# Masking the attention scores on VectorE in the operation that takes their minimum, with new plan prices and an earlier first w_oc blob

## The chip, the cores and the metric

The kernel runs on one core of a Trainium2 chip. A core has five engines that run their own instruction queues side by side: TensorE (PE in the profile; PEld is its weight loads), VectorE (DVE), ScalarE (ACT), GpSimd (POOL) and SyncE (SP), which here only issues transfers. They work on SBUF, TensorE writes its results to PSUM, and DMA engines move data between SBUF and HBM. The metric is the device time of one launch in microseconds (us), lower is better.

## What is computed

One decoder layer for 512 tokens of width 2048 in fp32: a modulation vector, a norm, one combined projection, a short convolution beside attention with 8 query heads in 2 key groups, an output projection, and a feed-forward part. The change lies in attention. Cut to what matters:

```python
def masked_softmax(s, mask):
    s = jnp.where(mask, s, jnp.finfo(jnp.float32).min)
    p = jax.nn.softmax(s, axis=-1)
    return jnp.where(mask, p, 0.0)
...
    # per block of 128 query rows; gathered and window branches, 8 heads each
    s = jnp.einsum('bgrqd,bgqkd->bgrqk', qbk, k_sel).astype(jnp.float32) * scale
    p = masked_softmax(s, (pos <= t[:, None])[:, :, None])
    o_slc = jnp.einsum('bgrqk,bgqkd->bgrqd', p.astype(v_sel.dtype), v_sel)
...
    s = jnp.einsum('bgrqd,bgkd->bgrqk', qbk, kw).astype(jnp.float32) * scale
    p = masked_softmax(s, wmask)
    o_win = jnp.einsum('bgrqk,bgkd->bgrqd', p.astype(vw.dtype), vw)
```

With 512 tokens the selection takes every block, and the window covers everything before it, so both branches have the same causal mask: key position not after the query row.

## The kernel before

The whole layer is one function, `hybrid_layer`, in three parts. Each part is recorded by a class `Order` instead of being issued at once: every call becomes a node with a price (`price`, lines 93 to 114, in us), and `emit` lays the nodes out in time by these prices, by their dependences and by the number of buffers, and then issues them in the order of planned start. Each engine works its own queue strictly in that order. So a wrong price does not change what is computed, but it changes which instruction stands behind which. All calls pass through line 122, so nearly all instructions carry that line in the profile, and one reads them by the names of their tiles.

1. The first plan (up to line 936): modulation (`w_ada` blobs, a multiply with a running sum on VectorE each, tile `t<-wa,cs`), projections, convolution, and the queries. `weights` (line 368) brings one weight blob of 512 KB: a transfer from SP's queue into `raw` (3 buffers), a copy to a rounded high half by ScalarE and a subtraction for the low half by VectorE into `wh` (2 buffers). TensorE computes each product as three products of halves (`mm3`).
2. The second plan (lines 948 to 1096): attention and the convolution's half of the output projection. This is where the change acts. `attention(g, qb)` handles one key group (2) and one block of 128 query rows (4): for two branches and four heads, three score products into a PSUM tile `s` (3 buffers), a fourth product that adds the causal mask to its last 128 columns (`s<-mask_r,ident_r`, line 995), the negated row maximum `nm` on VectorE (line 998), and on ScalarE the exponential into `p` with the row sum (line 1001). `p` is in SBUF with 8 buffers. That makes 64 such score tiles, 16 each of 128, 256, 384 and 512 columns. Then VectorE scales `p`, TensorE transposes it into `pt`, both others split it into `tt`, and TensorE multiplies with the values into `pv`. `out_conv(m)` (line 962), 16 times, is independent work: 24 products of 512 columns into `pw` with a blob of `w_oc`; the planner may put it wherever TensorE would idle, since it has the last place among the lanes (`lane(2)`). Query heads 4 to 7 (`head`, tiles `rt`, `q`) are rotated on VectorE among the first four blocks.
3. The third plan (from line 1101): the attention half of the output projection and the feed-forward part, tiles `pf`.

Between two plans nothing is planned: the second plan starts all engines at zero, whatever the first has left in their queues. `wanted()` marks nodes that are to be done 10 us before the first plan's end would ask for them. The price of a score maximum is taken from its output, one column, in the kernel before: 0.1 us at any width (line 106). The mask product is priced 0.06 us (line 101).

## Time and profile before

| | us |
|---|---|
| median of 3 runs (2114.53 to 2116.34) | 2115.92 |
| the profiled execution, whole | 2115.59 |
| its span, first to last instruction | 2113.8 |
| first score product of attention (start of the second plan's work on PE) | 554.25 |
| first product of the third plan | 759.22 |

| engine | busy us | share of the span |
|---|---|---|
| PE | 2068.4 | 98% |
| PEld | 1923.7 | 91% |
| DVE | 1885.7 | 89% |
| ACT | 1007.3 | 48% |
| POOL | 128.2 | 6% |

A product is written in the profile as its output tile, its two inputs and the columns that it streams. Products overlap, so the busy time of PE counts a product's latency too; how fast PE really goes is read from the distance between starts. A row of a window shows for each engine its busy time and number of instructions in that stretch, then the granted clock of TensorE as a share (1.00 is full), and the load of the DMA engines. The chain of waits follows the work that ended last back from the end, each step to what released it.

### The profile page before, as it was taken

Reading aid. Unit: us, or ns where it says so; the run is one execution under the profiler, and the core shown is the slowest. Engines: PE = TensorE matmul, PEld = TensorE weight load, DVE = VectorE, ACT = ScalarE, POOL = GpSimd, SP = SyncE. Lnnn points to the kernel's source line nnn. Section 1 sums busy time; section 2 is a strip of 40 time slices with the busy share of each in tenths; the row PEclk is TensorE's granted clock in tenths of the full one; section 3 lists DMA queues with packets and bytes.
Section 4 is the critical chain, followed back from the end, with each engine's and each line's share of the span. In section 5 each row is a group of like instructions: output and inputs, shape, how many; then the busy total and the mean of one; then the engine's idle time right before and its main releaser. Section 6 shows DMA issues by size and latency. Waiting matters only on the chain.

```text
span 2113.8 us, 38166 instructions
## 1 busy us (share of the span) xinstructions
PE 2068.4 (98%) x15070; PEld 1923.7 (91%) x15070; DVE 1885.7 (89%) x3039; ACT 1007.3 (48%) x1471; POOL 128.2 (6%) x244
## 2 busy tenths in 40 slices
PE   8999999999999999999999999999999999999997
PEld 6888787898777779999999999999999999999997
DVE  7999888888987556999999999999899999999997
ACT  5432433222455434766666666666444333334354
POOL 0000000000000001022211112111000000000000
PEclk8999999999999999999999999999999999999998
DMA  8897588888321144467666676668976466476442
GB/s 335 340 340 249 181 297 325 315 288 311 138 80 41 51 141 154 135 215 225 210 204 207 207 217 200 208 206 288 332 268 211 167 242 220 145 255 237 150 172 90
DMA packets 144130, 454.17 MB, mean 215 GB/s; under 512 B 15824, under 2 KB 20176, under 8 KB 143952
## 3 DMA queue, kind: packets, MB, share of 16 engines
q1 hardware_dynamic: 108816, 386.72, 53.0%
q0 software_dynamic: 34048, 63.98, 9.6%
q8 instruction: 118, 1.93, 0.4%
q10 hardware_dynamic: 1088, 1.05, 0.1%
q14 instruction: 60, 0.49, 0.1%
HBM read 383.53 MB, written 68.16 MB: 214 GB/s over the span
## 4 chain that ended last, share of the span: by engine, by line
PE 72%; DVE 9%; DMA 4%; ACT 2%; issue 2%; DVEq 0%; POOL 0%; SPq 0%; ACTq 0%
PE pf L122 55%; PE ps L122 11%; PE pw L122 3%; DMA rw<-in_w_f 1%; PE pv L122 1%; DVE hl L122 1%; DVE t L122 1%; DVE x L122 1%; PE s L122 1%; DMA wa<-in_w_ada 1%; PE pt L122 1%; DMA raw<-in_cmp_w 1%; DVE nm L122 1%; DVE wh L122 1%; DMA tk<-g 1%
## 5 line engine op out<-in xcount | busy, mean ns | idle before, releaser
L122 PE MATMUL pf<-tk,hl 128*128 128x256 f32 x10704 | 1223.3, 277 | 3.0 <-DVE hl L122 2.2
L122 PEld LDWEIGHTS pf<-tk,hl 128*128 128x128 f32 x10704 | 1219.9, 188 | 5.3 <-DVE hl L122 3.5
L122 ACT ACTIVATE hl<-rw 128x1024 fp32r<-128x1024 f32 x269 | 285.5, 1062 | 324.9 <-PE pf L122 280.1
L122 DVE TENSOR_TENSOR hl<-rw,hl 128x1024 fp32r<-128x1024 f32 (+2 forms) x351 | 336.5, 968 | 29.4 <-ACT hl L122 29.2
L122 ACT ACTIVATE hl<-sg 128x1024 fp32r<-128x1024 f32 x180 | 191.1, 1062 | 220.3 <-PE pf L122 172.8
L122 PE MATMUL ps<-h_m,wh 128*128 128x512 f32 x1080 | 252.0, 390 | 0.0
L122 DVE SCALAR_TENSOR_TENSOR t<-wa,cs 128x1024 bf16<-128x1024 f32 x192 | 234.5, 1221 | 16.1 <-DMA wa<-in_w_ada 13.8
L122 PEld LDWEIGHTS ps<-h_m,wh 128*128 128x128 f32 x1080 | 201.1, 188 | 41.5 <-DVE wh L122 0.3
L122 ACT ACTIVATE wh<-raw 128x1024 fp32r<-128x1024 f32 (+1 forms) x106 | 112.7, 1063 | 243.8 <-PE ps L122 215.7
L122 DVE TENSOR_TENSOR hl<-sg,hl 128x1024 fp32r<-128x1024 f32 (+2 forms) x193 | 188.1, 986 | 25.3 <-ACT hl L122 25.3
L122 PE MATMUL ps<-h,wh 128*128 128x512 f32 x840 | 198.7, 392 | 3.4 <-ACT h L122 2.3
L122 PEld LDWEIGHTS ps<-h,wh 128*128 128x128 f32 x840 | 157.7, 189 | 37.0 <-ACT h L122 2.7
L122 DVE TENSOR_TENSOR wh<-raw,wh 128x1024 fp32r<-128x1024 f32 (+1 forms) x106 | 129.9, 1225 | 21.2 <-ACT wh L122 19.9
L122 DVE TENSOR_TENSOR sg<-sg,rw 128x1024 f32<-128x1024 f32 x120 | 146.1, 1217 | 0.2
L122 DVE SCALAR_TENSOR_TENSOR x<-pf,mod,x 128x256 f32<-128x256 f32 (+1 forms) x280 | 131.8, 485 | 14.5 <-PE pf L122 12.8
L122 POOL DMA_DIRECT2D g<-gt x192 | 101.2, 532 | 379.7 <-ACT hl L122 222.1
L122 PE MATMUL pw<-mix,wh 128*128 128x512 f32 x384 | 109.7, 405 | 0.0
L122 DVE TENSOR_TENSOR sg<-rw 128x1024 f32<-128x1024 f32 x60 | 73.2, 1220 | 16.7 <-DMA rw<-in_w_f 14.0
L122 ACT ACTIVATE t<-t 128x512 f32<-128x512 f32 (+3 forms) x131 | 74.9, 572 | 21.1 <-DVE t L122 18.8
L122 PEld LDWEIGHTS pw<-mix,wh 128*128 128x128 f32 x384 | 69.6, 190 | 11.0 <-issue 0.5
L122 DVE TENSOR_TENSOR rw<-rw 128x1024 f32<-128x1024 f32 x60 | 73.0, 1217 | 0.0
L122 ACT ACTIVATE gt<-t 128x512 fp32r<-128x512 f32 x96 | 60.3, 630 | 22.6 <-DVE t L122 17.7
(215 smaller groups left out, 1802.1 us busy)
## 6 DMA issues: line engine op xcount, KB each, us to landing
rw<-in_w_f SPq DMA_DIRECT2D x263, 512.0 KB, 3.9
wa<-in_w_ada SPq DMA_DIRECT2D x192, 512.0 KB, 6.0
tk<-g SPq DMA_DIRECT2D x114, 512.0 KB, 6.2
g<-gt POOLq DMA_DIRECT2D x192, 256.0 KB, 4.1
raw<-in_w_conv SPq DMA_DIRECT2D x32, 512.0 KB, 4.3
x<-in_xt SPq DMA_DIRECT2D x16, 512.0 KB, 7.2
raw<-in_w_kv SPq DMA_DIRECT2D x16, 512.0 KB, 4.4
raw<-in_w_cv SPq DMA_DIRECT2D x16, 512.0 KB, 4.5
```

Of the source, the lines that this page charges most:

```text
L122: x.i, x.eng, x.call = len(self.nodes), eng, (lambda: real(*args, **kw))
```

## The change

The mask is no longer a product. A tile `causal` of 128 by 512 holds zeros and, in its last 128 columns, the causal mask; it is made in the first plan by a memset and a transfer. For each score tile VectorE adds the scores from PSUM and the fitting last columns of `causal`, negates the sum, writes it to `p` in SBUF and keeps the running minimum, which it writes to `nm`: two instructions, shown in the listings as ISA. ScalarE then takes the exponential in place, from `p` to `p`, with scale -1. The 64 mask products and the tiles `ident_r`, `mask_r` and `sr` go (the last becomes a temporary). The planner prices a product of the rounded kind at 0.1 us at least, and a reduction by its input's columns. The first blob of `w_oc` is asked for at the end of the first plan, under `wanted()`.

```diff
@@ price
-            return (0.109 if op == "transpose" else max(0.06, 0.0015 + n * 0.000453)), 0.2
+            return (0.109 if op == "transpose" else max(0.1, 0.0015 + n * 0.000453)), 0.2
...
+        if op == "tensor_reduce":
+            rows = max(Order.width(x) for x in ins)
+            return 0.068 + 0.00104 * rows * (1.7 if n > 16 else 1), 0.14
         if n < 16:
             return 0.1, 0.14
...
-        if op == "tensor_reduce":
-            n = max(Order.width(x) for x in ins) * (1.7 if n > 16 else 1)
         return 0.068 + 0.00104 * n, 0.14
@@ first plan
-            nc.sync.dma_start(out=cst, in_=a["cst"][:, C_MASK:])
+            nc.sync.dma_start(out=cst, in_=a["cst"][:, C_CMASK:])
+            nc.sync.dma_start(out=causal[:, T - P:], in_=a["cst"][:, C_MASK:C_CMASK])
...
-            nc.scalar.activation(ident_r, ident, AF.Copy)
-        if s == 18:
-            nc.scalar.activation(mask_r, cst[:, :C_CMASK - C_MASK], AF.Copy)
+            nc.vector.memset(causal[:, :T - P], 0.0)
...
+    with wanted():
+        first = [weights(a["w_oc"][0])]
@@ out_conv
-        wh, wl = weights(a["w_oc"][m])
+        wh, wl = first.pop() if first else weights(a["w_oc"][m])
@@ attention
-                    nc.tensor.matmul(s[:, w - P:w], ident_r, mask_r, start=False, stop=False)
...
-                nc.vector.tensor_reduce(out=nm[:, r:r + 1], in_=s[:, o:w], axis=AX.X, op=OP.max,
-                                        negate=True)
                 p = next(ps_)
-                nc.scalar.activation(p[:, :L], s[:, o:w], AF.Exp, bias=nm[:, r:r + 1],
+                nc.vector.tensor_tensor_reduce(out=p[:, :L], in0=s[:, o:w], in1=causal[:, T - L:], scale=-1.0,
+                                               scalar=BIG, op0=OP.add, op1=OP.min,
+                                               accum_out=nm[:, r:r + 1])
+                nc.scalar.activation(p[:, :L], p[:, :L], AF.Exp, bias=nm[:, r:r + 1], scale=-1.0,
                                      accum_out=sm[:, r:r + 1])
...
-        sr = next(srs)
+        sr = temp([P, P], name="sr")
```

The change also moves instructions, since the plan is made again. Three places follow, as listings of the two programs show them: the order of an engine's queue, without times, equal neighbours counted.

The first is TensorE where attention starts (`s` are scores, `pw` the convolution's output products, `pt` transposes). Before the change nothing but score and mask products stands between the last product of the first plan and these rows of TensorE's queue:

```order
L122 MATMUL s<-kwin,q 128x128
L122 MATMUL s<-mask_r,ident_r 128x128
L122 MATMUL s<-kwin,q 128x128 x3
L122 MATMUL s<-mask_r,ident_r 128x128
L122 MATMUL s<-kwin,q 128x128 x3
L122 MATMUL s<-mask_r,ident_r 128x128
L122 MATMUL s<-kwin,q 128x128 x2
L122 MATMUL pt<-vec,p 128x128 x2
L122 MATMUL pw<-mix,wh 128x512
```

The first `pw` product stood behind the first two transposes. After the change TensorE's queue reads, from the last products of the first plan (`ps`) on:

```order
L124 MATMUL ps<-h,wh 128x512 x84
L124 MATMUL s<-kslc_108,q 128x160 x9
L124 MATMUL pw<-mix,wh 128x512 x3
L124 MATMUL s<-kslc_108,q 128x160 x3
L124 MATMUL pw<-mix,wh 128x512 x4
L124 MATMUL s<-kwin,q 128x128 x9
L124 MATMUL pw<-mix,wh 128x512 x2
L124 MATMUL s<-kwin,q 128x128 x3
L124 MATMUL pw<-mix,wh 128x512
L124 MATMUL pt<-vec,p 128x128
```

Ten `pw` products have moved ahead of the first transpose, in four groups between the scores.

The second place is VectorE over the seam between the two plans (`t,late<-wa,cs` are sums over the last `w_ada` blobs, `wh<-raw,wh` the low half of a weight blob, `rt` the rotation of queries). VectorE's queue before the change:

```order
L122 TENSOR_TENSOR wh<-raw,wh 128x1024
L122 SCALAR_TENSOR_TENSOR t,late<-wa,cs 128x1024 x5
L122 TENSOR_TENSOR mod<-late 128x16
L122 TENSOR_TENSOR mod<-mod,vec 128x16
L122 MEMSET pc 128x96 x2
L122 TENSOR_TENSOR rt<-qr,rot 128x512
L122 TENSOR_REDUCE nm<-s 128x1
```

No blob of `w_oc` was split before attention started. VectorE's queue at the same place after the change:

```order
L124 TENSOR_TENSOR wh<-raw,wh 128x1024
L124 SCALAR_TENSOR_TENSOR t,late<-wa,cs 128x1024 x2
L124 TENSOR_TENSOR wh<-raw,wh 128x1024
L124 SCALAR_TENSOR_TENSOR t,late<-wa,cs 128x1024 x3
L124 TENSOR_TENSOR mod<-late 128x16
L124 TENSOR_TENSOR mod<-mod,vec 128x16
L124 MEMSET pc 128x96 x2
L124 TENSOR_TENSOR rt<-qr,rot 128x512
L124 ISA p,nm<-s,causal 128x128
L124 ISA nm 128x1
```

The low half of the first `w_oc` blob has moved ahead of the last three `w_ada` sums, and its transfer on SP's queue ahead of the last four `w_ada` transfers, behind all of which it stood before. Further on in VectorE's queue, 30 of the 64 new pairs are followed at once by the next pair.

The third place is TensorE at the end of the second plan (`pf` is the third). Before the change its queue ends so:

```order
L122 MATMUL pv<-tt,vv 128x512 x2
L122 MATMUL pw<-mix,wh 128x512 x9
L122 MATMUL pt<-ones,sr 128x1
L122 MATMUL pw<-mix,wh 128x512 x14
L122 MATMUL pt<-t,ones 128x512
L122 MATMUL pw<-mix,wh 128x512 x77
L122 MATMUL pf<-mixa,wh 128x512 x48
```

Behind the last value product stood 100 `pw` products. After the change the same end of TensorE's queue reads:

```order
L124 MATMUL pv<-tt,vv 128x512 x2
L124 MATMUL pw<-mix,wh 128x512 x9
L124 MATMUL pt<-ones,t 128x1
L124 MATMUL pw<-mix,wh 128x512 x9
L124 MATMUL pt<-t,ones 128x512
L124 MATMUL pw<-mix,wh 128x512 x46
L124 MATMUL pf<-mixa,wh 128x512 x48
```

Now 64 stand there: 36 have moved forward, in among the softmax work. The order of the third plan's products is the same in both programs.

## The prediction

> **What bounds the kernel now.** I read the page's chain of waits first. By engine it says:

> ```profile
> PE 72%; DVE 9%; DMA 4%; ACT 2%; issue 2%; DVEq 0%; POOL 0%; SPq 0%; ACTq 0%
> ```

> TensorE sets most of the time, so what goes from its queue counts, unless another engine leads at that place. The change acts between 554 and 759 us; the windows of that stretch come next (busy time of PE, PEld, DVE, ACT, POOL, then the granted clock):

> ```profile
> 540.00:550.00 10.00, 10.00 (x46) 8.29 (x45) 9.90 (x16) 1.12 (x2) 0.00 (x0) 1.00 0.33 107
> 550.00:560.00 10.00, 8.12 (x48) 6.83 (x46) 8.53 (x26) 4.79 (x13) 0.00 (x0) 1.00 0.82 312
> 560.00:570.00 10.00, 9.26 (x46) 8.46 (x46) 8.32 (x30) 5.51 (x19) 0.00 (x0) 0.66 0.19 56
> ...
> 554.25:605.00 50.75, 45.90 (x237) 36.59 (x236) 46.43 (x135) 26.62 (x79) 0.00 (x0) 0.93 0.23 80
> 605.00:741.88 136.88, 134.16 (x708) 105.52 (x707) 94.81 (x224) 66.35 (x167) 0.00 (x0) 1.00 0.19 61
> ```

> Up to 605 VectorE is busy 46.43 of 50.75 us and TensorE has holes; from 605 to 742 TensorE is busy 134.16 of 136.88 and VectorE has 42 us to spare. The chain in order of time, asked for this stretch, agrees: steps of VectorE at first, at the end one long run of `pw`:

> ```profile
> 572.60 1.05 DVE p L122 x4
> ...
> 577.40 0.60 DVE rt L122
> 578.00 0.98 DVE sr L122
> ...
> 741.88 17.50 PE pw L122 x77
> ```

> So the first quarter is VectorE's, the rest TensorE's, and 77 `pw` products wait at the end that could have filled holes.

> **The mask products.** Their price on TensorE is read from distances of starts, in the timeline of PE:

> ```profile
> 597.27 0.22 PE L122 MATMUL s<-mask_r,ident_r 128*128 128x128 f32 x1
> 597.33 0.92 PE L122 MATMUL s<-kslc,q 128*128 128x512 f32 x3
> 598.08 0.22 PE L122 MATMUL s<-mask_r,ident_r 128*128 128x128 f32 x1
> 598.14 0.91 PE L122 MATMUL s<-kslc,q 128*128 128x512 f32 x3
> 598.89 0.22 PE L122 MATMUL s<-mask_r,ident_r 128*128 128x128 f32 x1
> ...
> 741.32 18.06 PE L122 MATMUL pw<-mix,wh 128*128 128x512 f32 x77
> 759.22 1.07 PE L122 MATMUL pf<-mixa,wh 128*128 128x512 f32 x4
> ```

> From mask to mask it is (598.89 - 597.27) / 2 = 0.81 us for three products of 512 columns and one mask. A product of 512 takes (759.22 - 741.32) / 77 = 0.2325, three take 0.70, so a mask costs 0.11, and 64 of them **7.2 us**. 32 belong to the first key group, where VectorE leads; there the gain is real only if `pw` products take their place, which is counted under the prices below.

> **The hole at the start, and the clock.** These rows of the timeline lie around 554 us:

> ```profile
> 543.35 1.06 ACT L122 ACTIVATE wh<-raw 128x1024 fp32r<-128x1024 f32 x1 [3.29 <-PE ps L122]
> 552.41 2.64 ACT L122 ACTIVATE qr<-ps 128x512 f32<-128x512 f32 x4 [8.00 <-PE ps L122]
> 553.76 1.23 DVE L122 SCALAR_TENSOR_TENSOR t<-wa,cs 128x1024 bf16<-128x1024 f32 x1 [1.26 <-DMA wa<-in_w_ada]
> 557.07 0.19 PEld L122 LDWEIGHTS s<-kslc,q 128*128 128x128 f32 x1 [1.51 <-ACT p L122]
> 560.79 0.69 PE L122 MATMUL pt<-vec,p 128*128 128x128 f32 x2 [0.74 <-DVE p L122]
> 561.14 0.78 PE L122 MATMUL pw<-mix,wh 128*128 128x512 f32 x1
> 561.24 1.22 DVE L122 TENSOR_TENSOR wh<-raw,wh 128x1024 fp32r<-128x1024 f32 x1
> ```

> From 554.25 to 560.79 TensorE had only 24 score and 8 mask products, at 0.11 each (128 to 160 columns, like the mask) 3.5 of 6.5 us; the rest it waited, for ScalarE to free score tiles among others. Now 24 scores and ten `pw` products stand there, 24 x 0.11 + 10 x 0.2325 = 5.0 us: **1.4 us** more work in the hole, besides what replaces its masks. Is their blob ready? ScalarE idles for 8.00 us ahead of 552.41, and VectorE waits 1.26 us for the last `w_ada` transfer just where the new split stands, so the 1.22 us of the split fill that wait, and the row at 561.24 leaves VectorE's busiest stretch. If the blob's transfer of 512 KB delays that `w_ada` transfer in full, at the 312 GB/s of the window that is 1.7 us more wait; from none to 1.7, I take 0.4, since the blob goes out when the `w_ada` queue still waits for buffers.

> The window from 560 to 570 has a granted clock of 0.66: it lost 10 x 0.34 = 3.4 us of TensorE. It follows the hole. With 5.0 us of products there in place of 3.5, I expect the clock to stay up: **3.4 us**. [...]

> **The new operation on VectorE.** No run shows it. The nearest rows are the reduction it replaces, the same kind of sum from PSUM and SBUF, and the running sum with its read-out:

> ```profile
> L122 DVE TENSOR_REDUCE nm<-s 128x1 f32<-128x512 f32 x16 | 11.0, 685 | 1.2 <-PE s L122 1.2
> L122 DVE TENSOR_REDUCE nm<-s 128x1 f32<-128x128 f32 x16 | 4.2, 280 | 0.9 <-PE s L122 0.8
> L122 DVE TENSOR_TENSOR pc<-s,cst 128x128 f32<-128x128 f32 x2 | 0.6, 294 | 0.1
> ...
> L122 DVE TENSOR_TENSOR part<-ps,part 128x512 f32<-128x512 f32 x32 | 19.8, 683 | 0.7 <-PE ps L122 0.7
> ...
> L122 DVE SCALAR_TENSOR_TENSOR t<-wa,cs 128x1024 bf16<-128x1024 f32 x192 | 234.5, 1221 | 16.1 <-DMA wa<-in_w_ada 13.8
> ...
> 543.92 1.22 DVE L122 SCALAR_TENSOR_TENSOR t<-wa,cs 128x1024 bf16<-128x1024 f32 x1
> 545.06 0.08 DVE L122 DVE_READ_ACCUMULATOR t<-wa,cs 128x1 f32 x1
> 545.18 1.23 DVE L122 SCALAR_TENSOR_TENSOR t<-wa,cs 128x1024 bf16<-128x1024 f32 x1
> 546.33 0.08 DVE L122 DVE_READ_ACCUMULATOR t<-wa,cs 128x1 f32 x1
> 546.33 1.22 DVE L122 TENSOR_TENSOR wh<-raw,wh 128x1024 fp32r<-128x1024 f32 x1
> ```

> Sum and reduction cost the same, 683 and 685 at 512 columns, 294 and 280 at 128. A running result beside the sum costs nothing at 1024 columns, but its read-out holds up the next one of its kind: 545.18 - 543.92 = 1.26, against 546.33 - 545.18 = 1.15 where a plain operation follows, so 0.11 or nothing. Low end: the reduction's price. High end: a sum and a reduction one after the other, about 0.49 us more (mean over the four widths, from 0.29 at 128 to 0.68 at 512). I take the read-out alone, as it is nearest in kind: 30 of the 64 stand back to back, 30 x 0.11 = 3.3 us, half of them in the first key group, which is where VectorE leads: **1.7 us** on the path, less the 1.2 that left, plus the 0.4 of above. The other half falls into the 42 idle us.

> [...]

> **The prices.** A reduction of 512 columns was planned at 0.1 us and took 0.685; now it is planned near its time. 36 `pw` products (8.4 us) move forward, ten of them counted. The other 26 are 6.0 us. The 24 masks of the first group that are left took 2.6; beyond their place 3.4 can fill waits. If they fill nothing where VectorE leads, the 2.6 of the masks are lost again; between 2.6 lost and 3.4 won I take **1.0** won, near the middle, since TensorE is busy 45.90 of 50.75 and 134.16 of 136.88 us and so has some holes in both stretches. The first plan keeps its order save a memset, two small ScalarE copies and a split transfer, hidden by TensorE (10.00 of 10.00 from 540 to 550); the third keeps it whole.

> **ScalarE** now reads SBUF:

> ```profile
> L122 ACT ACTIVATE gt<-t 128x512 fp32r<-128x512 f32 x96 | 60.3, 630 | 22.6 <-DVE t L122 17.7 <-DMA g<-gt 4.0
> ...
> L122 ACT ACTIVATE tt<-pt 128x512 fp32r<-128x512 f32 x48 | 28.6, 596 | 54.4 <-PE pt L122 54.2
> ```

> That is 34 ns more for each of 64, 2.2 us, beside 66.35 busy of 136.88: nothing on the path. In return a score tile is free once VectorE is through.

> Sum: -7.2 - 1.4 - 3.4 - 1.0 + 1.7 - 1.2 + 0.4 = **-12.1**. From the profiled execution's 2115.59 (0.33 below the median of the runs) that is **2103.5**.

> **Rivals.** *Only the masks go.* The order waits for VectorE at the start as before, the clock drops again: -7.2 + 0.9, about 2109. For it: the second plan starts with VectorE's queue of 2 us still unworked, so the fourth score tile waits anyway.

> *More is filled.* All 26 moved products find holes (2.4 more) and the read-outs hide (1.7): 2099.4, and less where other waits shrink with them.

> *The wait for `p` changes engine.* The waits of the second plan have this row:

> ```profile
> ACT p L122 <- PE pt L122: 15.4, 9, 2.6
> ```

> ScalarE waited for transposes to free `p`. Now VectorE writes `p` first and waits in its place, and behind it stand the `tt` splits that TensorE's value products need. Were most of it, say 12 us, on the path, the gain is gone: 2115.5. Against it: the planner knows the buffers, and VectorE has idle time there.

> *The operation is slow* (the one that ends slower). Its place is VectorE's first quarter with 32 of the tiles, its price the high end above: 32 x 0.49 = 15.7 us on the path, and a third of as much in the second group, 5 (42.7 tiles' worth in all): 2103.5 + 20.7 = 2124. It decides from 12.1 / 42.7 = 0.28 us per tile on. [...]

> **Chances.** The forecast, 2101 to 2107, 0.42; only the masks, 2107 to 2111, 0.20; more filled, 2094 to 2101, 0.16; the wait for `p` 0.10; half rate 0.05; slower still 0.04; between these 0.03. A measurement can tell about 0.2% (4.2 us) from no change. Faster by that holds the first three, 0.78; within it lie the wait for `p`, most of half rate and the rest, 0.16; slower 0.06. The range 2095 to 2116 leaves out the slow operation at both prices, the edge of the wait for `p` and of the more filled, under 0.2.

> **What would show it.** Right: 64 fewer products; pairs of 0.29 and 0.69 us at 128 and 512 columns; `pw` ahead of the first `pt`; a clock of 1.00 from 550 to 580; the first `pf` near 747. Wrong: longer pairs, VectorE waiting for `pt` at `p`, or a clock drop that stays.

## The result, and the profile after

| | before | after |
|---|---|---|
| median of six runs (lowest to highest), us | 2116.13 (2110.08 to 2120.42) | 2099.36 (2090.91 to 2105.6) |
| span of the profiled execution, us | 2113.8 | 2103.8 |
| first score product | 554.25 | 558.62 |
| first `pf` product (end of the second plan on TensorE) | 759.22 | 747.66 |
| from the first score to the first `pf` (called the stage below) | 204.97 | 189.04 |

The ratio is 0.9918, with an interval of 0.9896 to 0.9939: about 17 us faster. The profiled execution is the longest of its six, so its own time (2105.6) understates the gain. On the page of the changed kernel the chain of waits by engine has more TensorE and less VectorE than before (72% and 9% there):

```profile
PE 76%; DVE 7%; DMA 3%; ACT 2%; issue 1%; DVEq 0%; ACTq 0%; SPq 0%
```

The windows of the changed kernel, with the same columns as before: ten microseconds at the start of attention, the first quarter (50.75 us from the first score), the rest of the softmax work up to the last `pw` products, the last stretch ahead of the first `pf`, and the whole stage:

```profile
560.00:570.00 10.00, 8.45 (x35) 6.84 (x34) 9.04 (x45) 4.28 (x16) 0.00 (x0) 0.69 0.60 225
...
558.62:609.37 50.75, 49.20 (x250) 40.54 (x249) 47.22 (x165) 29.38 (x84) 0.00 (x0) 0.93 0.27 96
609.37:734.90 125.53, 125.53 (x659) 99.83 (x658) 95.56 (x265) 66.24 (x163) 0.00 (x0) 1.00 0.21 69
734.90:747.66 12.76, 11.49 (x49) 8.85 (x48) 12.65 (x20) 8.03 (x12) 0.00 (x0) 1.00 0.00 1
...
558.62:747.67 189.05, 186.23 (x956) 149.23 (x954) 155.44 (x446) 103.64 (x258) 0.00 (x0) 0.98 0.21 71
```

In the first quarter TensorE is now busy 49.20 us, with 45.90 before, and in the middle for all of 125.53. But the granted clock at the start is 0.69: in this execution the drop stayed. And a new place shows at the end: in the last 12.76 us VectorE is full (12.65) and TensorE has a hole. The timeline of PE of the same kernel names both places:

```profile
558.62 1.13 PE L124 MATMUL s<-kslc,q 128*128 128x160 f32 x9
559.58 0.91 PE L124 MATMUL pw<-mix,wh 128*128 128x512 f32 x3
561.98 0.56 PE L124 MATMUL s<-kslc,q 128*128 128x160 f32 x3 [1.49 <-DVE pc L124]
562.38 1.11 PE L124 MATMUL pw<-mix,wh 128*128 128x512 f32 x4
...
747.66 0.70 PE L124 MATMUL pf<-mixa,wh 128*128 128x512 f32 x2 [1.27 <-DVE x L124]
749.36 10.73 PE L124 MATMUL pf<-mixa,wh 128*128 128x512 f32 x46 [1.00 <-DVE wh L124]
```

The `pw` products stand in the hole at the start, as the new order has them, and TensorE still waits 1.49 us for VectorE there. At the seam to the third plan it waits 1.27 and 1.00 us for VectorE (`x` is the residual, `wh` the low half of the next blob), where before the first `pf` stood straight behind `pw`.

The new operation has these rows among the groups of VectorE, and in its timeline, where pairs stand back to back (the trace writes the operation and its read-out under the names `CUSTOM_DVE_ANT_0` and `DVE_READ_ACCUMULATOR2_ANT`):

```profile
L124 DVE CUSTOM_DVE_ANT_0 p<-s,causal 128x512 f32<-128x512 f32 x16 | 10.4, 686 | 1.9 <-PE pt L124 1.9
L124 DVE CUSTOM_DVE_ANT_0 p<-s,causal 128x128 f32<-128x128 f32 x16 | 4.1, 283 | 1.0 <-PE pt L124 0.7 <-PE s L124 0.2
...
562.67 0.29 DVE L124 CUSTOM_DVE_ANT_0 p<-s,causal 128x128 f32<-128x128 f32 x1
562.89 0.08 DVE L124 DVE_READ_ACCUMULATOR2_ANT nm<- 128x1 f32 x1
562.89 0.28 DVE L124 CUSTOM_DVE_ANT_0 p<-s,causal 128x128 f32<-128x128 f32 x1
563.10 0.08 DVE L124 DVE_READ_ACCUMULATOR2_ANT nm<- 128x1 f32 x1
563.10 0.28 DVE L124 CUSTOM_DVE_ANT_0 p<-s,causal 128x128 f32<-128x128 f32 x1
```

686 and 283 ns are the durations of the reduction that went (685 and 280). From pair to pair it is 562.89 - 562.67 = 0.22 and 0.21 us, less than one operation's length: the read-out holds up nothing here. Last, the waits of the stage, three rows of the changed kernel, asked from 553 to 760 us (us in total, times, longest):

```profile
PEld pv L124 <- DVE tt L124: 4.5, 21, 0.4
...
ACT p L124 <- DVE nm L124: 10.7, 16, 2.4
...
DVE p L124 <- PE pt L124: 3.4, 4, 0.9
```

The wait for transposes that free `p` was 15.4 us on ScalarE and is 3.4 on VectorE; in return ScalarE's exponentials now wait 10.7 us for VectorE's pairs. TensorE's value products waited for VectorE's `tt` much longer before, as the same view of the kernel before shows:

```profile
PEld pv L122 <- DVE tt L122: 14.0, 33, 1.1
```

### The profile page after: what moved, and what is told of

It reads as the page before. It is cut to its first block, busy times and chain, and to the rows that moved or that the text cites. A ratio compares the mean times of both kernels' runs of the same rounds, so it can differ in the third digit from the quotient of the medians.

```text
span 2103.8 us, 38070 instructions
## 1 busy us (share of the span) xinstructions
PE 2060.6 (98%) x15006; PEld 1918.9 (91%) x15006; DVE 1886.2 (90%) x3104; ACT 1009.8 (48%) x1469; POOL 128.2 (6%) x244
## 3 DMA queue, kind: packets, MB, share of 16 engines
q10 hardware_dynamic: 1088, 1.05, 0.1%
## 4 chain that ended last, share of the span: by engine, by line
PE 76%; DVE 7%; DMA 3%; ACT 2%; issue 1%; DVEq 0%; ACTq 0%; SPq 0%
PE pf L124 56%; PE ps L124 11%; PE pw L124 4%; PE pv L124 2%; PE s L124 2%; DVE t L124 1%; DVE hl L124 1%; PE pt L124 1%; DVE x L124 1%; DMA raw<-in_cmp_w 1%; DMA rw<-in_w_f 1%; DMA wa<-in_w_ada 1%; DMA tk<-g 1%; DVE tk L124 1%; DVE wh L124 1%
```

## The experiments

Twelve kernels ran in three groups, each group on one chip beside the kernel before, whose medians were 2118.38, 2116.26 and 2117.49 us. All ratios are to the kernel before of the same group, with their 95% intervals; 0.001 is 2.1 us, and an interval reaches about 3 us to either side. First scores come between 554 and 560 us in the single profiles, and the order of the first plan's products doesn't explain it: the changed kernel's profiles have 558.62, 556.83 and 558.12, and a kernel with the same first plan (the one whose second plan starts VectorE at 1.9 us, below) 554.70. So from profiles the stages are compared, not the spans.

### One part at a time

The first group has the three parts of the change. Only the operation: the changed kernel with the old prices and without the early blob. (The operation is itself priced by its columns even there, since `tensor_tensor_reduce` falls through to the last line of `price`.)

```diff
-            return (0.109 if op == "transpose" else max(0.1, 0.0015 + n * 0.000453)), 0.2
+            return (0.109 if op == "transpose" else max(0.06, 0.0015 + n * 0.000453)), 0.2
...
-        if op == "tensor_reduce":
-            rows = max(Order.width(x) for x in ins)
-            return 0.068 + 0.00104 * rows * (1.7 if n > 16 else 1), 0.14
...
-    with wanted():
-        first = [weights(a["w_oc"][0])]
...
-        wh, wl = first.pop() if first else weights(a["w_oc"][m])
+        wh, wl = weights(a["w_oc"][m])
```

> The new operation alone: old prices, no early w_oc blob. The operation itself is priced by its width even so. Terms theory (each part by its own term): masks 7.2 gone, little else, so about 7 below the kernel before, attention stage (first score product to first pf) near 197. Plan theory (the excess came from a plan that knows VectorE's time for the maximum): the operation brings its own right price, so 13 to 16 below, stage near 190. Release theory (score tiles freed by VectorE instead of ScalarE): also 13 to 16 below; told from the plan theory by op_cheap and prices_only.

Measured: 2107.78 us, ratio 0.9949 (0.9936 to 0.9961), 10.6 us faster: between the 7 of the terms theory and the 13 to 16 of the other two.

Only the prices: the kernel before, masks kept, with the new lines of `price`.

```diff
-            return (0.109 if op == "transpose" else max(0.06, 0.0015 + n * 0.000453)), 0.2
+            return (0.109 if op == "transpose" else max(0.1, 0.0015 + n * 0.000453)), 0.2
...
+        if op == "tensor_reduce":
+            rows = max(Order.width(x) for x in ins)
+            return 0.068 + 0.00104 * rows * (1.7 if n > 16 else 1), 0.14
...
```

> The kernel before with the new prices alone, mask products kept. Terms theory: within 1 of before. Plan theory: the maximum is planned at its time, so the waits of TensorE in the stage shrink by 6 to 9 and the time falls as much. Release theory: within 1 of before, as ScalarE still frees the score tiles.

Measured: 2107.46 us, ratio 0.9948 (0.9935 to 0.9960), 10.9 us faster. All 64 mask products are still there, so this gain owes nothing to them, and ScalarE still frees the score tiles: the release theory, which expected no change here, falls. In its profile the gain lies in the stage, which takes 194.42 us in place of 204.97.

Only the early blob: the kernel before with `wanted()` around the first `w_oc` blob.

```diff
+    with wanted():
+        first = [weights(a["w_oc"][0])]
...
-        wh, wl = weights(a["w_oc"][m])
+        wh, wl = first.pop() if first else weights(a["w_oc"][m])
```

> The kernel before with the early w_oc blob alone. Terms theory: 1.4 below, 4.8 if the clock stays up at the start of attention. Plan and release theories: 1 to 2 below, the clock falls there as in the changed kernel, since the hole before the first transposes is still mostly waits.

Measured: 2114.38 us, ratio 0.9984 (0.9973 to 0.9995), 3 to 4 us faster. The parts alone sum to 25 us, the change has 17. The operation alone and the prices alone both bring a true price for the maximum of a score tile, so it is counted twice. Within the change that price comes with the operation, which is priced by its columns whether or not the new lines of `price` are there.

### What the price of the maximum is worth

The changed kernel, whole, with one line that prices the new operation at 0.1 us, as the maximum was priced before:

```diff
-        if n < 16:
+        if n < 16 or op == "tensor_tensor_reduce":
             return 0.1, 0.14
```

> The whole change, but the new operation planned at 0.1 us like the old maximum. Terms theory: like the changed kernel within 1.5. Plan theory: the gain beyond the masks is lost, 6 to 9 above the changed kernel, stage near 196. Release theory: like the changed kernel, stage near 189.

Measured: 2110.6 us, ratio 0.9961 (0.9949 to 0.9974). The change was measured three times (with the result, and in the second and the third group) and had 0.9918, 0.9929 and 0.9914, so this one wrong number gives back 0.9961 - 0.9920 = 0.0041, about 9 us. The stage agrees: 199.13 us against 189.04 in the change's first profile, and both have the clock drop. The other way round, the kernel before with the price of `tensor_reduce` alone, the 0.06 of a mask product kept:

```diff
+        if op == "tensor_reduce":
+            rows = max(Order.width(x) for x in ins)
+            return 0.068 + 0.00104 * rows * (1.7 if n > 16 else 1), 0.14
...
```

> The kernel before with one of the two new prices, that of a reduction by its input's columns; products of the rounded kind stay at 0.06 at least. If the price of the maximum is what the plan lacked: like prices_only, 9 to 12 below before. If the price of the small products is: within 2 of before.

Measured: 2108.54 us, ratio 0.9965 (0.9953 to 0.9977), 7.7 us faster. It carries most of what the prices bring; its interval and that of all the prices (0.9935 to 0.9960) overlap, so the small products' price stays at a few us or nothing.

How does a price do this? The prediction had counted `pw` products that move forward. The windows, asked for tile `pw` alone (busy time and number of PE, PEld, DVE), from the first score to just behind the last value product, give that count: the kernel before, then the kernel with the prices alone:

```profile
554.25:735.60 181.35, 86.21 (x286) 51.30 (x287) 8.20 (x11) 0.98 0.20 66
```

```profile
554.86:726.90 172.04, 86.72 (x291) 51.89 (x292) 8.93 (x12) 0.98 0.19 71
```

Only 5 more `pw` products stand in it, and yet the stretch is 9.3 us shorter. The same rows of the change with the cheap price, then of the change itself:

```profile
555.27:737.40 182.13, 95.28 (x321) 58.34 (x322) 9.66 (x13) 0.98 0.19 68
```

```profile
558.62:730.70 172.08, 94.87 (x321) 58.08 (x322) 9.67 (x13) 0.98 0.22 73
```

The same 321 products, the same mean clock, and 10.1 us between them. So the gain isn't in the number of products that fill, but in what stands behind what. The waits of the weight loads in the change with the cheap price say for whom TensorE waited:

```profile
PEld pv L124 <- DVE tt L124: 11.0, 35, 1.1
...
PEld s L124 <- DVE nm L124: 6.7, 12, 2.3
```

In the change these are 4.5 and 1.2:

```profile
PEld s L124 <- DVE nm L124: 1.2, 6, 0.2
```

The kernel with the prices alone, masks and all, shows the same against the 14.0 of the kernel before:

```profile
PEld pv L123 <- DVE tt L123: 2.8, 14, 0.2
```

This wait sorts all the profiles by the plan's price, whatever else was changed in them:

| VectorE's work on a score tile is priced | TensorE's wait for VectorE's `tt`, us |
|---|---|
| at 0.1 us: the kernel before, the early blob alone, the change with the cheap price | 14.0, 11.5, 11.0 |
| by its columns: the prices alone, the reduction's price alone, the operation alone, the change without the blob, the change (three profiles), with the extra product, with VectorE planned to start later (two kernels) | 2.8, 3.1, 5.2, 4.8, 4.5 each, 3.7, 4.7 and 4.9 |

With the cheap price the plan issues scores before VectorE has freed their tiles, and puts VectorE's pairs in fewer and longer groups (28 groups of the 64 pairs, the last four of four pairs each; 34 in the change), behind which `tt` is late. That much of the order is seen; which single displacement costs how much was not taken apart.

### What a mask product is worth

The changed kernel with one product more per score tile, of 128 columns, where the mask product stood; its scores count one of the three half products twice in their last 128 columns.

```diff
+                    nc.tensor.matmul(s[:, w - P:w], q[:, 0, qc], kt[:, 1, c0 + w - P:c0 + w], start=False, stop=False)
```

> The changed kernel with one more product of 128 columns in each of the 64 score tiles, in the place of the mask product; it adds the low half of the keys for the last 128 columns a second time, so those scores are off by a rounding-sized term. If a mask product on TensorE was worth its issue time: 7 above the changed kernel, stage near 196, work of TensorE 184. If the waits in the stage take it up: within 2 of the changed kernel.

Beside it, in the same group, the changed kernel itself:

> The changed kernel once more, to stand beside the three others on one chip: 15 to 18 below the kernel before, stage near 189 of which 177 is work of TensorE.

Measured: 2105.41 us, ratio 0.9951 (0.9937 to 0.9965), against 2100.56 and 0.9929 (0.9914 to 0.9944) for the change: 4.8 us for 64 products, 0.076 each, between the 7 and the 2 of the expectation. The distance of starts had given 0.11. The two intervals overlap a little, so the price could lie some 3 us to either side.

### What VectorE's time per tile is worth

The changed kernel with its order on every engine untouched, and one maximum of 128 columns of `p` with itself, in place, issued behind each pair; the plan doesn't know of it.

```diff
             ins = self.tc.keep_in_program_order(nodes[i].call())
+            if i in self.again:
+                eng, o = self.again[i]
+                self.tc.keep_in_program_order(eng.tensor_tensor(out=o, in0=o, in1=o, op=OP.max))
```

> The changed kernel, its order on every engine untouched, with one operation more on VectorE behind each of the 64 pairs, that the plan does not know of: a maximum of the first 128 columns of p with itself, in place, about 0.22 to 0.29 us each (64 x 0.25 = 16 us of VectorE). The prediction held that VectorE leads in the first quarter, so that a time per tile counts there in full and by a third in the second group (42.7 tiles' worth): 42.7 x 0.25 = about +11 us, back near the kernel before, ratio 0.998. The rival says that with the reduction planned at its true price the order leaves waiting room and products stand in between, so VectorE's time per tile is mostly covered: +3 us or less, ratio 0.994 or lower. Or worse than the first: exponentials behind the pairs get late too, +16 us and more, ratio over 1.000.

Measured: 2117.95 us, ratio 1.0000 (0.9990 to 1.0011), against 2100.24 for the change in the same group: 17.7 us slower, more than the 11 expected, and the whole gain gone. That is the third case of the expectation, in which the exponentials get late too. Its rows: the group of the added operation, and the timeline of VectorE with three pairs in a row:

```profile
L197 DVE TENSOR_TENSOR p<-p 128x128 f32<-128x128 f32 x64 | 18.7, 292 | 2.2
...
561.78 0.28 DVE L125 CUSTOM_DVE_ANT_0 p<-s,causal 128x128 f32<-128x128 f32 x1
561.99 0.08 DVE L125 DVE_READ_ACCUMULATOR2_ANT nm<- 128x1 f32 x1
562.11 0.29 DVE L197 TENSOR_TENSOR p<-p 128x128 f32<-128x128 f32 x1
562.32 0.28 DVE L125 CUSTOM_DVE_ANT_0 p<-s,causal 128x128 f32<-128x128 f32 x1
```

From pair to pair it is now 562.32 - 561.78 = 0.54 us in place of 0.21, so 0.33 per tile, 21 us for 64; of these 17.7 came out at the end, 54 tiles' worth. VectorE's time per tile, where the plan does not know of it, counts almost in full over the whole stage, although its busy share was 155.44 of 189.05 us there. Two things are in that weight. TensorE's wait for `tt` is back at 14.5 us, as in the plans with the cheap price. And the added operation writes `p`, so that the exponential of the tile has to wait for it: ScalarE's waits for it sum to 21.5 us, where in the change it waited 10.7 for the pairs.

```profile
ACT p L125 <- DVE p L197: 21.5, 21, 3.4
```

The run does not tell VectorE's time from this longer chain. The windows of this kernel, first quarter and rest, show both engines short of full:

```profile
556.27:607.02 50.75, 46.38 (x225) 35.51 (x224) 48.94 (x177) 26.32 (x78) 0.00 (x0) 0.93 0.25 89
607.02:743.78 136.76, 132.69 (x663) 99.25 (x662) 109.39 (x309) 68.39 (x162) 0.00 (x0) 1.00 0.17 58
```

In the rest VectorE has 27 us to spare and still delays TensorE, since the pairs stand ahead of the steps that TensorE asks for next. This stage also had the clock drop, which the change's profile in this group did not. Against the change's first profile, which had it too, the stage is 15.8 us longer (204.85 and 189.04).

### The early blob, and the hole at the start

The changed kernel without the early blob:

```diff
-    with wanted():
-        first = [weights(a["w_oc"][0])]
...
-        wh, wl = first.pop() if first else weights(a["w_oc"][m])
+        wh, wl = weights(a["w_oc"][m])
```

> The changed kernel without the early first w_oc blob: the operation and the plan's prices. If the blob's parts of the sum hold (a fuller start, 1.2 us of split off VectorE's busiest stretch, and the clock), it is 3 to 6 us slower than the changed kernel, ratio 0.995 against 0.9925. If the blob only moves a wait, as the kernel with the blob alone (ratio 0.998) leaves possible, it is within 2 us of the changed kernel.

Measured: 2104.93 us, ratio 0.9936 (0.9921 to 0.9952). The change itself, once more, in this group:

> The changed kernel once more, on the same chip as these three, for their comparison: 2100 to 2101 us, ratio 0.992 to 0.993. If the clock drop at the start of attention depends on the execution, the profile may have it or not; with it the stage from the first score product to the first product of the third plan takes about 189 us, without it 185.7.

Measured: 2100.24 us, ratio 0.9914 (0.9901 to 0.9928). So the blob is worth 4.7 us within the change, again with intervals that overlap a little. Two of the change's three profiles have no clock drop at the start. The window from 560 to 570 of the change in the second group, then of the change without the blob:

```profile
560.00:570.00 10.00, 9.96 (x60) 8.17 (x60) 9.90 (x53) 7.13 (x25) 0.00 (x0) 1.00 0.34 121
```

```profile
560.00:570.00 10.00, 10.00 (x50) 8.63 (x51) 9.62 (x45) 6.27 (x21) 0.00 (x0) 0.84 0.33 107
```

But the two profiles of the change without this drop have one at the seam to the third plan instead, behind the two waits for VectorE. The window there in the third group's profile, and its `pf` products, which took 10.73 us in the profile of the result and take 12.35 here:

```profile
745.00:750.00 5.00, 4.73 (x14) 3.72 (x15) 1.35 (x2) 0.00 (x0) 0.00 (x0) 0.66 0.00 0
...
745.27 12.35 PE L124 MATMUL pf<-mixa,wh 128*128 128x512 f32 x46 [1.00 <-DVE wh L124]
```

So about 1.7 us of the 3.4 that the clock gave at the start were lost again there (5 x 0.34).

Then the blind spot that the second plan starts all engines at zero. The changed kernel with VectorE starting at 1.9 us and ScalarE at 0.8, about what the first plan leaves them:

```diff
+        free.update(self.backlog)
...
+    order.backlog = {"vector": 1.9, "scalar": 0.8}
```

> The changed kernel with one thing more: the second plan starts VectorE at 1.9 us and ScalarE at 0.8 us in place of zero, about what the first plan leaves in their queues. If the waits for VectorE that are left at the start of attention (1.49 and 1.01 us in the profile of the changed kernel) and the clock drop behind them come from that blind spot, 2 to 4 us faster, ratio 0.991. If what is won there is given back at the seam to the third plan, where VectorE is full, the same as the changed kernel, ratio 0.9925.

Measured: 2096.49 us, ratio 0.9901 (0.9885 to 0.9916), the fastest here, 3.8 us under the change in its group; the intervals overlap, so it isn't settled that it beats the change, only the kernel before. The profiles do not put the 3.8 us where the edit acts: of the 4.5 us between the profiled spans of the change in this group and this kernel (2098.4 and 2093.9), 0.5 lie in the stage (185.45 and 184.93) and 3.4 ahead of the first score (558.12 and 554.70), where the two programs are the same. The start itself is closed: between the first score and the first transpose the timeline of PE names no wait, and the window reads

```profile
560.00:570.00 10.00, 10.00 (x62) 8.82 (x61) 10.00 (x49) 6.85 (x22) 0.00 (x0) 1.00 0.17 66
```

The seam to the third plan has its waits as before, VectorE's `x` and `wh`:

```profile
739.63 0.70 PE L125 MATMUL pf<-mixa,wh 128*128 128x512 f32 x2 [1.42 <-DVE x L125]
741.33 12.18 PE L125 MATMUL pf<-mixa,wh 128*128 128x512 f32 x46 [1.00 <-DVE wh L125]
```

An attempt on that seam, in the second group, was the same with the first two `w_oa` blobs of the third plan asked for earlier as well:

```diff
+    order.backlog = {"vector": 1.9, "scalar": 0.8}
...
-    oa = [weights(a["w_oa"][k]) for k in range(2)]
+    with wanted():
+        oa = [weights(a["w_oa"][k]) for k in range(2)]
```

> The changed kernel with two more things told to the plans: the second plan starts VectorE at 1.9 us and ScalarE at 0.8 (what they still had in their queues when attention began), and the first two blobs of w_oa are asked for early, as the first of w_oc is. If unworked queues at the two seams cost TensorE its waits there: 3 to 6 below the changed kernel, no clock drop at the start of attention, under 1 us of wait ahead of the first two runs of pf. If not: within 2.

Measured: 2101.34 us, ratio 0.9933 (0.9919 to 0.9948), no better than the change (0.9929). One wait for VectorE's `x` of 3.69 us stands at the seam of its profile: in VectorE's timeline a split of `wh` (1.22 us from 745.02) now stands right ahead of `x` (746.15), where VectorE is full.

## Why the prediction was right in sign and short in size

It said 2103.5 us; 2099.36 came, inside the range of 2095 to 2116, and beyond the likeliest case's own (2101 to 2107), in that of the rival *more is filled* (2094 to 2101). The single terms were further off than the total: the masks were put 2.4 us too high, the blob 0.9 too high and the prices 8 too low. That the total came within about 4 us is in part luck, since these errors partly cancel. Term by term, in us of the whole time:

| term | predicted | measured | by |
|---|---|---|---|
| 64 mask products | -7.2 | -4.8 | the extra product |
| early blob: fuller start -1.4, clock -3.4, split -1.2, transfer +0.4 | -5.6 | -4.7 | the change without the blob |
| plan's prices, the new operation's among them | -1.0 | about -9 | the operation priced at 0.1 |
| read-out of the running minimum | +1.7 | 0 | pairs 0.21 us apart |
| all | -12.1 | -16.8 | the runs of the change |

Each measured term was taken with the others in place and has an interval of some 3 us to either side; together they make 18.5.

**The mask products** brought a gain as said, though at two thirds of their size: 4.8 would be near what remains if the 32 in the first quarter, where VectorE leads, were worth half of the others (5.3), which was not tried. **The early blob** was about right. Within it, the clock was not: it was forecast to stay at 1.00, and in the change's profiles it did so twice and not the third time. Each of the five profiled kernels without the early blob had a drop at the start of attention (0.66 from 560 to 570 us in the kernel before and 0.84 in the change without the blob, 0.93 over the first quarter with the prices alone); of the nine profiles with it four had one (the change's first, the cheap price, the extra product, the added operation: 0.66 to 0.69 from 560 to 570 us) and five had none. That fits a fuller start that makes the drop less frequent rather than impossible, but with one execution per profile it isn't shown. And where it stayed away in the change, a shorter one came at the seam. The hole isn't closed: 1.49 us of waiting for VectorE are left there, where the plan believes VectorE free.

**The step that failed is that on the prices.** It took 36 `pw` products that move forward, found that 26 of them could fill 6.0 us, took off the 2.6 of the masks' place, and bounded the gain at 3.4. The bound was false because the measure was: with equal numbers of `pw` products ahead of the last value product (321 and 321) the stretch differs by 10.1 us. A price that is up to seven times too low (0.1 for 0.685) on the engine that leads puts VectorE's queue into a wrong sequence, and the waits that vanish with the true price are those for `tt` (14.0 to 4.5 us in the change, 2.8 with the prices alone), not only holes that `pw` fills. The row with 14.0 was there to be read before; it is the size that the bound should have been made from.

**The read-out** was sized by the accumulating rows of the sums over `w_ada`, which hold each other up by 0.11 us. The new operation does not (0.21 us from pair to pair, at 283 ns for the operation alone): nearest in kind was not the same thing.

**The rivals.** *Only the masks go* falls: the other parts bring more than the masks do. *More is filled* named 2099.4, and that is where the time came, but only part of its reason holds: the read-outs hide and, as it added, other waits shrink; the 2.4 us by further `pw` products do not explain the gain, since the cheap price moves as many forward and lacks it. The agreement to 0.1 us is luck. *The wait for `p` changes engine* did happen, at 3.4 us in place of 15.4, and no loss was seen from it. *The operation is slow* falls by its rows, 283 and 686 ns. Half rate, which the chances put at 0.05, is shown by no run: the new operation, whose scores come from PSUM, ran at the reduction's 1.05 ns per column ((686 - 283) / 384). What the rival said of the point from which the change loses holds: 0.28 us per tile was predicted at a gain of 12.1 and a weight of 42.7 tiles; at 0.33 us per tile the measured gain of 17 is gone, with a weight of 54 (48 by the stages of the two profiles with a drop). **ScalarE** pays 23 to 30 ns per exponential from SBUF, which were forecast at 34 (369 ns became 392 at 128 columns, 694 became 724 at 512, by the groups of ScalarE in the two profiles); whether any of it is on the path was not tried alone.

## What to carry to other kernels

Where an order is made from prices, compare each price with the measured duration first, on the engine that leads above all: one number that was too low by a factor of up to seven was worth more here, by the medians, than 64 instructions (about 9 us and 4.8). Size a new order by the waits it can remove, for the leading engine's steps (here `pv<-tt`), not by how many filler instructions change place. And read the busy share of the second engine with care: VectorE at 82% of the stage delayed the end by 84% of what was added to each of its tiles behind the plan's back. What the same time costs when the plan knows of it was not tried.

## What the runs showed of the hardware that had not been expected

```profile
561.74 0.08 DVE L124 DVE_READ_ACCUMULATOR2_ANT nm<- 128x1 f32 x1
561.74 0.18 DVE L124 TENSOR_TENSOR pc<-s,cst 128x32 f32<-128x32 f32 x1
```

The added maximum, which reads the tile that the pair has just written, starts 0.12 us behind the read-out instead (561.99 and 562.11 in the rows above), and so adds 0.33 us and not 0.21. That the shared tile is the reason was not tried apart.

The drop of the granted clock at the start of attention differs between executions of one kernel: 0.69 from 560 to 570 us in one of the change, 1.00 in two, with waits for VectorE of 1.49, 1.01 and 0.93 us ahead of it. Asked in steps of 0.5 us, the clock stands at 0.50 during a drop, for 6.8 us in the kernel before and in this profile of the change, and for 3.4 us in the change without the blob (a mean of 0.84 over the 10 us from 560 and 0.99 over the 10 before) and at the seam in the change's other two profiles (a mean of 0.66 over the 5 us from 745 in the third group's). The profile of the change with the longest of those waits, 1.49 us, is the one with the drop at the start, but what starts a drop these runs do not show.
